# A hybrid decoder block on one core: the recurrence projected ahead of the convolution branch, two convolutions and ten weight tiles moved behind the opening of the last scan

## The chip, the core and the metric

The kernel runs on one core of a Trainium2 chip. The metric is device time in microseconds (us), from launch to end of one execution. Engines by their names in the profile: PE (matrix multiply; PEld is its weight load), DVE (vector), ACT (activations), POOL, and SP, which here only issues DMAs.

## The reference, cut to what matters

528 positions (16 learned ones and 512 of the input) with 1024 channels, one layer. `p = h @ W_in` has columns for three users:

```python
y_conv = conformer_conv(p[..., :2048], ...)      # GLU, causal depthwise conv of 31 taps, LayerNorm, silu, @ w_conv_out
y_rwkv = rwkv7_time_mix(p[..., 2048:5408], ...)  # 16 heads; S_t = S_{t-1} diag(w_t) + (S_{t-1} a_t) b_t^T + v_t k_t^T
gates  = sigmoid(p[..., 5408:] + b_gate)         # 2 x 1024 columns
y = gates[..., :1024] * y_conv + gates[..., 1024:] * y_rwkv
h = layer_norm(ALPHA * h + y @ w_o, ln1_g, ln1_b)
h = layer_norm(ALPHA * h + conv_gated_mlp(h, ffn_up, ffn_dw, ffn_down), ln2_g, ln2_b)
```

All of it is float32.

## The kernel before

Activations lie channels by positions, 128 channels to a tile. A product keeps float32 accuracy by three matmuls: weights and activations are each split into a high and a low part (`wh`, `wl`; `hhi`, `hlo`), and `gemm` (L167) sums high x high, low x high and high x low into one PSUM bank, for 8 blocks of 128 input channels. So one weight tile (128 output columns) against one half of the positions is 24 matmuls of 256 to 272 columns. A weight tile is loaded by SP into `wr` (two buffers), ACT writes `wh` (L153), DVE writes `wl` (L154). PSUM has eight banks: three `ps_g`, two `ps_x`, two `ps_a`, one `ps_m`.

The first phase works through steps that the string `SCHEDULE` (L50) names in program order. For a pair p of heads: `K` projects k, v, r (three weight tiles); `P` prepares the decays, keys and the matrices `Gt`; `S` (L505) inverts the triangular blocks in `Gt` by 61 dependent DVE instructions (L543 to L549), with a DRAM round trip on either side; `C` merges the inverse (L571) and runs the scan (L604), 9 dependent steps of small matmuls and copies through two `ps_x` banks; `F` (L647) normalises the scan's output in `ps_x` banks too and writes it to `o_dr`. For a channel tile j: `G` (L701) makes the GLU with two weight tiles; the convolution (L724) is 48 DVE instructions, either in between the steps of a solve (`S01`: solve of pair 0 with convolution 1) or by itself at low priority (`T`); it ends in `c_dr`. `A` (L751) makes one of 16 gate tiles with one weight tile and writes it to `g_dr`. `N` runs `conv_norm` (L768), the LayerNorm over channels of the convolution's output, which needs all eight tiles.

The string sets priorities and not the order. A planner orders each engine's instructions ahead of time: of those that could run by its own costs, the one first in program order goes first. `front()` puts instructions ahead of everything, `back()` behind, and `behind(ins, first)` forces one instruction behind another. On the chip each engine then runs its list in order. Weight preparation, the reads of PSUM after a `gemm`, and the scan are in `front()`. So PE, whenever the scan waits, takes matmuls from later `K`, `G` or `A` steps, if their inputs and buffers are there.

After the first phase: `w_conv_out` against the normalised convolution, times the first eight gates, to `ya_dr` (L834 to L844); `w_rwkv_out` against the scan's output, loaded from `o_dr` through two buffers, times the other eight gates, plus `ya` (L855 to L878); `w_o` in two halves of the positions, each followed by the first LayerNorm (L887 to L919); the up projection, 44 weight tiles (L932); the down projection (L981), which sums in all eight banks.

The functions that the diff touches, as they stand before:

Of the kernel before, what the change touches and what calls it, by code (L numbers as in the profile page):

```python
# [2 lines left out]

# [1 line left out]

# [37 lines left out]
GN_EPS = 64e-5  # L43
EXPM05 = float(np.exp(-0.5))
BACK = 3000
NKEEP = 6
GW = 132


SCHEDULE = ("G0 K0 P0 T0 G1 S01 K1 P1 C0 K2 F0 G2 S12 K3 P2 C1 G3 F1 K4 S23 G4 P3 C2 F2 A S34 K5 P4 C3 F3 G5 S4 A "  # L50
            "T5 K6 P5 G6 C4 F4 S56 P6 C5 K7 F5 G7 S67 A A A P7 C6 F6 S7 A A C7 A A N A A A A A A A F7")


@with_exitstack
def hybrid_block(ctx: ExitStack, tc: tile.TileContext, a, out, dbg=None):
# [108 lines left out]
    def wload(dram, c0, wpool=None, bufs=2):  # L164
        return wsplit(wcols(dram, c0), [P, NK, P], wpool, bufs)

    def gemm(ps, w, xh, xl, sl, nk=NK):  # L167
        wh, wl = w
        for k in range(nk):
            TE.matmul(ps, wh[:, k, :], xh(k, sl), start=(k == 0), stop=False)  # L170
            TE.matmul(ps, wl[:, k, :], xh(k, sl), start=False, stop=False)  # L171
            TE.matmul(ps, wh[:, k, :], xl(k, sl), start=False, stop=(k == nk - 1))  # L172

    hh = lambda k, sl: hhi[:, k, sl]
    hl = lambda k, sl: hlo[:, k, sl]
# [633 lines left out]
    for step in SCHEDULE.split():  # L809
        what, p, q = step[0], int(step[1:2] or 0), int(step[2:] or -1)  # L810
        if what == "K":
            raw[p] = rkv(p)
        elif what == "P":
            prs[p] = prep(p, *raw.pop(p))
        elif what == "S":
            solved[p] = solve(prs[p], conv(q, cpads.pop(q)) if q >= 0 else ())
        elif what == "C":
            with front():
                merge(prs[p], *solved[p])
                ys[p] = chain(prs[p])  # L820
        elif what == "F":
            finish(prs[p], ys.pop(p))
        elif what == "G":
            cpads[p] = glu(p)
        elif what == "T":
            with back():
                for _ in conv(p, cpads.pop(p)):
                    pass
        elif what == "A":
            gate(gates.pop(0))  # L830
        elif what == "N":
            ctx_a1.close()
            rb, zh, zl = conv_norm()
    for j in range(NK):  # L834
        ga = rb.tile([P, NQ], F32, name="ga", bufs=2)
        nc.sync.dma_start(out=ga, in_=g_dr[j])
        w = wload(a["w_conv_out"][0], P * j)
        for sl, n in qsl:
            pt = gbank()
            gemm(pt[:, :n], w, lambda k, s: zh[k][:, s], lambda k, s: zl[k][:, s], sl)  # L840
# [3 lines left out]
        nc.sync.dma_start(out=ya_dr[j], in_=ga)  # L844
    ctx_b1.close()
    ctx_a2.close()


    ctx_b2, ctx_o = ExitStack(), ExitStack()
    op = pool(ctx_o, "rout", "left")  # L850
    mp = pool(ctx_b2, "mix", "right")
    ot = lambda dt, name: op.tile([P, NQ], dt, name=name, tag="ot", bufs=16)
    yt = lambda dt, name: mp.tile([P, NQ], dt, name=name, tag="yt", bufs=16)
    oh, ol, yh, yl = [], [], [], []
    for j in range(NK):  # L855
        o_t = op.tile([P, NQ], F32, name="o_t", bufs=2)
        nc.sync.dma_start(out=o_t, in_=o_dr[j])
        oh.append(ot(F32R, "oh"))
        ol.append(ot(F32R, "ol"))
        split(oh[j], ol[j], o_t)  # L860
    for j in range(NK):
        gb_ = op.tile([P, NQ], F32, name="gb_", bufs=2)
        nc.sync.dma_start(out=gb_, in_=g_dr[8 + j])
        ya = op.tile([P, NQ], F32, name="ya", bufs=2)
        nc.sync.dma_start(out=ya, in_=ya_dr[j])
        w = wload(a["w_rwkv_out"][0], P * j)
        yh.append(yt(F32R, "yh"))
        yl.append(yt(F32R, "yl"))
        for sl, n in qsl:
            pt = gbank()  # L870
            gemm(pt[:, :n], w, lambda k, s: oh[k][:, s], lambda k, s: ol[k][:, s], sl)
            with front():
                V.scalar_tensor_tensor(out=gb_[:, sl], in0=gb_[:, sl], scalar=1.0, in1=pt[:, :n],
                                       op0=ALU.add, op1=ALU.mult)
# [12 lines left out]
    for (t0, t1), (sl, n) in zip(QH, qsl):  # L887
        pm, pv = abank(), abank()
        xs = []
        s1, s2 = half_tile("s1", n, 1), half_tile("s2", n, 1)  # L890
        for j in range(NK):
            w = kept[j] if j < NKEEP else wload(a["w_o"][0], P * j)
            pt = gbank()
            gemm(pt[:, :n], w, lambda k, s: yh[k][:, s], lambda k, s: yl[k][:, s], sl)
            x1 = half_tile("x1", n, 10)
            with front():
                V.scalar_tensor_tensor(out=x1, in0=hlo[:, j, t0:t1].bitcast(F32), scalar=ALPHA,
                                       in1=pt[:, :n], op0=ALU.mult, op1=ALU.add)
# [6 lines left out]
        with front():  # L905
# [7 lines left out]
            rs1 = mp.tile([P, 258], F32, name="rs1")[:, :n]  # L913
# [18 lines left out]
    def up_block(js):  # L932
# [107 lines left out]
```

## Time and profile before

| | |
|---|---|
| runs, us | 1180.61, 1184.78, 1188.44; median 1184.78 |
| profiled execution, us | 1186.58, its span 1184.5 |
| PE busy | 1131.2 us, 95% |
| DVE busy | 863.1 us, 73% |
| ACT busy | 565.0 us, 48% |
| mean granted PE clock | 0.979 of 2.4 GHz |

Times in the rows are microseconds from the start of the span; the first phase reaches to about 680, the two output projections to 750, the LayerNorm to 820, the up projection to 1057. Matmuls are pipelined: a busy PE can still be waiting inside, so the count of matmuls in a stretch is read beside its busy time.

### The profile page before, as it was taken

Reading aid. Unit: us, or ns where it says so; the run is one execution under the profiler, and the core shown is the slowest. Engines: PE = TensorE matmul, PEld = TensorE weight load, DVE = VectorE, ACT = ScalarE, POOL = GpSimd, SP = SyncE. Lnnn points to the kernel's source line nnn. Section 1 sums busy time; section 2 is a strip of 40 time slices with the busy share of each in tenths; the row PEclk is TensorE's granted clock in tenths of the full one; section 3 lists DMA queues with packets and bytes.
Section 4 is the critical chain, followed back from the end, with each engine's and each line's share of the span. In section 5 each row is a group of like instructions: output and inputs, shape, how many; then the busy total and the mean of one; then the engine's idle time right before and its main releaser. Section 6 shows DMA issues by size and latency. Waiting matters only on the chain.

```text
span 1184.5 us, 22671 instructions
## 1 busy us (share of the span) xinstructions
PE 1131.2 (95%) x8718; PEld 1066.5 (90%) x8718; DVE 863.1 (73%) x2179; ACT 565.0 (48%) x1211; POOL 83.2 (7%) x242
## 2 busy tenths in 40 slices
PE   5999999999999999999988999999999999999997
PEld 4998989899898989988977989998999999998885
DVE  6598999879898998976496447798876666652227
ACT  5644456537566565655585433346433443432120
POOL 6001010102101110101000000000000000000000
PEclk9999999999999999999898989999999999999999
DMA  5333342423414153344442376522332323343321
GB/s 161 86 89 91 86 95 63 93 57 90 100 55 107 42 108 81 80 119 107 128 134 77 98 223 191 166 71 75 105 106 74 107 74 106 90 137 95 94 84 71
DMA packets 202438, 118.99 MB, mean 100 GB/s; under 512 B 50036, under 2 KB 186397, under 8 KB 202331
## 3 DMA queue, kind: packets, MB, share of 16 engines
q1 hardware_dynamic: 182992, 113.81, 34.3%
q10 hardware_dynamic: 17515, 3.17, 1.5%
q8 instruction: 68, 1.11, 0.4%
q0 software_dynamic: 1824, 0.57, 0.3%
q14 instruction: 39, 0.32, 0.1%
HBM read 102.24 MB, written 15.28 MB: 99 GB/s over the span
## 4 chain that ended last, share of the span: by engine, by line
PE 64%; DVE 8%; DMA 5%; ACT 2%; issue 2%; POOL 0%; ACTq 0%; SPq 0%; DVEq 0%; POOLq 0%
PE ps_g L170 14%; PE ps_g L171 14%; PE ps_g L172 14%; PE ps_x L607 7%; PE psf L984 3%; PE psf L986 3%; PE psf L985 3%; DMA t22s<-dT 1%; PE ps_a L473 1%; PE ps_m L594 1%; DVE wl L154 1%; DMA dT<-W 1%; DMA t<-dT 1%; DMA wr<-in_ffn_up_dram 1%; DMA o_t<-o_dr 1%
## 5 line engine op out<-in xcount | busy, mean ns | idle before, releaser
L170 PE MATMUL ps_g<-hhi,wh 128*128 128x256 f32 (+2 forms) x1648 | 478.2, 290 | 4.7 <-DVE v L210 2.1
L171 PE MATMUL ps_g<-hhi,wl 128*128 128x256 f32 (+2 forms) x1648 | 478.2, 290 | 0.0
L172 PE MATMUL ps_g<-hlo,wh 128*128 128x256 f32 (+2 forms) x1648 | 476.2, 289 | 0.0
L170 PEld LDWEIGHTS ps_g<-hhi,wh 128*128 128x128 f32 x1648 | 314.1, 191 | 7.5 <-DVE v L210 2.5
L171 PEld LDWEIGHTS ps_g<-hhi,wl 128*128 128x128 f32 x1648 | 313.4, 190 | 2.8 <-issue 0.8
L172 PEld LDWEIGHTS ps_g<-hlo,wh 128*128 128x128 f32 x1648 | 314.0, 191 | 1.6 <-issue 0.6
L154 DVE TENSOR_TENSOR wl<-wr,wh 128x1024 fp32r<-128x1024 f32 x151 | 183.9, 1219 | 96.1 <-ACT wh L153 95.7
L153 ACT CAST wh<-wr 128x1024 fp32r<-128x1024 f32 x151 | 158.0, 1047 | 119.5 <-PE psf L985 75.2
L745 DVE SCALAR_TENSOR_TENSOR cev<-cd,drv,cev 128x257 f32<-128x257 f32 x216 | 99.0, 477 | 0.1
L942 ACT COPY pu<-ps_g 128x258 f32<-128x258 f32 (+1 forms) x88 | 32.8, 373 | 110.6 <-PE ps_g L172 110.6
L607 PE MATMUL ps_x<-UV,Gt 128*66 128x64 f32 (+1 forms) x576 | 71.1, 246 | 2.7 <-DMA Gt<-dT 2.3
L607 PEld LDWEIGHTS ps_x<-UV,Gt 128*66 128x66 f32 (+1 forms) x576 | 65.6, 168 | 4.4 <-DMA Gt<-dT 2.5
L984 PE MATMUL psf<-wh,hidh 128*128 128x512 f32 x176 | 69.3, 394 | 0.0
L986 PE MATMUL psf<-wl,hidh 128*128 128x512 f32 x176 | 69.0, 392 | 0.0
L985 PE MATMUL psf<-wh,hidl 128*128 128x512 f32 x176 | 68.3, 388 | 0.0
L949 DVE SCALAR_TENSOR_TENSOR u<-pu,prm,u 128x512 f32<-128x512 f32 x88 | 65.6, 747 | 1.3
L737 DVE SCALAR_TENSOR_TENSOR csh<-cpad,drv,csh 128x257 f32<-128x257 f32 x120 | 57.3, 477 | 0.5
L638 DVE SCALAR_TENSOR_TENSOR Sb<-Sb,lc,ps_x 64x64 f32<-64x64 f32 x112 | 31.3, 280 | 30.8 <-PE ps_x L607 29.2
L947 DVE TENSOR_SCALAR u<-pu,prm 128x512 f32<-128x512 f32 x44 | 21.2, 484 | 43.5 <-ACT pu L942 43.5
L547 DVE TENSOR_TENSOR stmp<-L,W 128x60 f32<-128x60 f32 (+21 forms) x216 | 45.1, 209 | 1.3
L549 DVE TENSOR_TENSOR W<-W,stmp 128x60 f32<-128x60 f32 (+21 forms) x216 | 45.0, 208 | 1.0
L170 PE MATMUL ps_g<-zh,wh 128*128 128x258 f32 (+1 forms) x128 | 38.4, 302 | 7.6 <-ACT zh L138 7.6
(308 smaller groups left out, 1992.2 us busy)
## 6 DMA issues: line engine op xcount, KB each, us to landing
wr<-in_w_in_dram SPq DMA_DIRECT2D x59, 512.0 KB, 4.3
wr<-in_ffn_up_dram SPq DMA_DIRECT2D x44, 512.0 KB, 4.0
wr<-in_ffn_down_dram SPq DMA_DIRECT2D x22, 512.0 KB, 3.6
wr<-in_w_o_dram SPq DMA_DIRECT2D x10, 512.0 KB, 4.4
g_dr<-gt SPq DMA_DIRECT2D x16, 257.0 KB, 3.0
L<-dA SPq DMA_DIRECT2D x32, 128.0 KB, 3.9
wr<-in_w_conv_out_dram SPq DMA_DIRECT2D x8, 512.0 KB, 4.2
wr<-in_w_rwkv_out_dram SPq DMA_DIRECT2D x8, 512.0 KB, 5.9
```

What stands on the lines that cost most here:

```text
L153: first = S.copy(out=hi, in_=raw)
L154: V.tensor_tensor(out=lo, in0=raw, in1=hi.bitcast(F32), op=ALU.subtract)
L170: TE.matmul(ps, wh[:, k, :], xh(k, sl), start=(k == 0), stop=False)
L171: TE.matmul(ps, wl[:, k, :], xh(k, sl), start=False, stop=False)
L172: TE.matmul(ps, wh[:, k, :], xl(k, sl), start=False, stop=(k == nk - 1))
L607: mm = lambda o, l, r, start: TE.matmul(o, l, r, start=start, stop=True, skip_group_check=True)
L737: yield V.scalar_tensor_tensor(out=cs_, in0=x1[:, i:i + NM], scalar=dcol(D_SCW, 8 * i + j) if i < HT else dcol(D_HCW, 8 * 2 * i + j), in1= ...
L745: yield V.scalar_tensor_tensor(out=yp[:, b, :] if lasttap else ev[:, b, :], in0=d[:, i:i + NM], scalar=dcol(D_HCW, 8 * (2 * i + b) + j), i ...
L949: V.scalar_tensor_tensor(out=u, in0=p_[:, t:t + SEQ], scalar=pcol(C_FW, 44 * t + m), in1=u, op0=ALU.mult, op1=ALU.add)
L984: TE.matmul(acc[t][d], hidh[:, k, ts], wd[k][0][:, ds], start=(k == 0), stop=False)
L985: TE.matmul(acc[t][d], hidl[:, k, ts], wd[k][0][:, ds], start=False, stop=False)
L986: TE.matmul(acc[t][d], hidh[:, k, ts], wd[k][1][:, ds], start=False, stop=(k == NF - 1))
```

## The change

The string: convolutions 0 to 5 stand in the solve of their own pair (`S00` to `S55`), 6 and 7 after everything of the last pair (`U6`, `U7`, at plain priority). `H` notes the first matmul of the last scan; from there to the end of the string every `gemm` puts its first matmul behind that one. Behind `H` stand the GLU tiles 6 and 7 and the last eight gates, four of them behind `U7`. `w_rwkv_out` comes next and writes gated `ya_dr`; then `conv_norm`; then `w_conv_out`, which adds `ya`. In these two stages the first two weight tiles are multiplied together, input block by input block, into four banks; the same is done for the second half of the positions in the up projection. The banks of a stage are taken in turn from `ps_g` and `ps_x`, or `ps_g` and `ps_a`. The scan's output gets 17 buffers in place of two for its loads. In the first LayerNorm `hhi + hlo` is added ahead of the product. Five tiles of `w_o` are kept for the second half, not six.

```diff
-NKEEP = 6
+NKEEP = 5
-SCHEDULE = ("G0 K0 P0 T0 G1 S01 K1 P1 C0 K2 F0 G2 S12 K3 P2 C1 G3 F1 K4 S23 G4 P3 C2 F2 A S34 K5 P4 C3 F3 G5 S4 A "
-            "T5 K6 P5 G6 C4 F4 S56 P6 C5 K7 F5 G7 S67 A A A P7 C6 F6 S7 A A C7 A A N A A A A A A A F7")
+SCHEDULE = ("G0 K0 P0 S00 K1 G1 P1 C0 K2 F0 S11 K3 P2 C1 G2 F1 K4 S22 P3 C2 G3 F2 A K5 S33 P4 C3 G4 F3 A K6 S44 P5 C4 "
+            "G5 F4 K7 S55 P6 C5 A F5 A S6 P7 C6 A F6 A S7 A A C7 H G6 G7 A A A A F7 U6 U7 A A A A")
+    hold = []
     def gemm(ps, w, xh, xl, sl, nk=NK):
         wh, wl = w
         for k in range(nk):
-            TE.matmul(ps, wh[:, k, :], xh(k, sl), start=(k == 0), stop=False)
+            first = TE.matmul(ps, wh[:, k, :], xh(k, sl), start=(k == 0), stop=False)
+            if k == 0 and hold:
+                behind(first, hold[-1], "work kept for the scan's waits")
...
+    def gemms(jobs, xh, xl, nk=NK):
+        for k in range(nk):
+            for ps, (wh, wl), sl in jobs:
+                TE.matmul(ps, wh[:, k, :], xh(k, sl), start=(k == 0), stop=False)
+                TE.matmul(ps, wl[:, k, :], xh(k, sl), start=False, stop=False)
+                TE.matmul(ps, wh[:, k, :], xl(k, sl), start=False, stop=(k == nk - 1))
+    turn, turn_a = cycle((gbank, xbank, gbank, xbank, gbank)), cycle((gbank, abank, gbank, abank, gbank))
+    obank = lambda: next(turn)()
+    cbank = lambda: next(turn_a)()
...
-        keys(X, 0, True)
+        opening = keys(X, 0, True)
...
+        elif what == "U":
+            for _ in conv(p, cpads.pop(p)):
+                pass
+        elif what == "H":
+            hold.append(opening)
...
+    ot = lambda dt, name: op.tile([P, NQ], dt, name=name, tag="ot", bufs=17)
...
+    for j in range(NK):
+        o_ts.append(ot(F32, "o_t"))
+        nc.sync.dma_start(out=o_ts[j], in_=o_dr[j])
...
+        if j < 2:
+            if j == 0:
+                first = [wload(a["w_rwkv_out"][0], P * i) for i in range(2)]
+                banks = [[obank()[:, :n] for sl, n in qsl] for i in range(2)]
+                gemms([(banks[i][x], first[i], qsl[x][0]) for i in range(2) for x in range(2)],
+                      lambda k, s: oh[k][:, s], lambda k, s: ol[k][:, s])
...
+        nc.sync.dma_start(out=ya_dr[j], in_=gb_)
+    ctx_a1.close()
+    rb, zh, zl = conv_norm()
...
-            V.tensor_tensor(out=ya[:, sl], in0=ya[:, sl], in1=gb_[:, sl], op=ALU.add)
+            V.tensor_tensor(out=ya[:, sl], in0=ya[:, sl], in1=ga[:, sl], op=ALU.add)
...
-            pt = gbank()
+            pt = obank()
+            x1 = half_tile("x1", n, 12)
+            V.tensor_tensor(out=x1, in0=hhi[:, j, t0:t1].bitcast(F32), in1=hlo[:, j, t0:t1].bitcast(F32), op=ALU.add)
             gemm(pt[:, :n], w, lambda k, s: yh[k][:, s], lambda k, s: yl[k][:, s], sl)
-            x1 = half_tile("x1", n, 10)
             with front():
-                V.scalar_tensor_tensor(out=x1, in0=hlo[:, j, t0:t1].bitcast(F32), scalar=ALPHA,
-                                       in1=pt[:, :n], op0=ALU.mult, op1=ALU.add)
-                V.scalar_tensor_tensor(out=x1, in0=hhi[:, j, t0:t1].bitcast(F32), scalar=ALPHA,
-                                       in1=x1, op0=ALU.mult, op1=ALU.add)
+                V.scalar_tensor_tensor(out=x1, in0=x1, scalar=ALPHA, in1=pt[:, :n], op0=ALU.mult, op1=ALU.add)
...
-        for sl, n in qsl:
-            for x in ws:
-                pt = gbank()
-                gemm(pt[:, :n], wt[x], lambda k, s: h1h[:, k, s], lambda k, s: h1l[:, k, s], sl)
+        for i_, (sl, n) in enumerate(qsl):
+            pts = [obank() for x in ws]
+            jobs = [(pt[:, :n], wt[x], sl) for pt, x in zip(pts, ws)]
+            for some in [jobs] if i_ else [[job] for job in jobs]:
+                gemms(some, lambda k, s: h1h[:, k, s], lambda k, s: h1l[:, k, s])
```

## Rows read from the trace of the kernel before

**Rows 1.** Stretches: length; busy (count) of PE, PEld, DVE, ACT, POOL; clock, DMA, GB/s

```profile
60.00:500.00 440.00, 429.70 (x3496) 404.08 (x3495) 396.43 (x1242) 248.39 (x597) 51.29 (x140) 0.98 0.33 82
500.00:608.00 108.00, 104.40 (x844) 96.74 (x844) 73.02 (x249) 65.22 (x165) 7.50 (x23) 0.95 0.46 119
600.00:640.00 40.00, 29.24 (x210) 27.68 (x210) 34.58 (x94) 29.23 (x58) 1.69 (x2) 0.83 0.28 77
618.00:632.00 14.00, 5.22 (x22) 4.58 (x21) 13.86 (x39) 9.19 (x15) 0.00 (x0) 0.57 0.12 37
640.00:680.00 40.00, 40.00 (x341) 37.80 (x341) 17.09 (x45) 18.09 (x45) 0.00 (x0) 1.00 0.37 117
680.00:720.00 40.00, 37.09 (x284) 36.45 (x283) 20.32 (x37) 13.34 (x20) 0.00 (x0) 0.91 0.74 218
776.00:824.00 48.00, 43.27 (x349) 42.17 (x348) 41.09 (x92) 27.10 (x60) 0.00 (x0) 1.00 0.19 54
820.00:840.00 20.00, 20.00 (x171) 20.00 (x170) 18.49 (x26) 10.74 (x17) 0.00 (x0) 1.00 0.46 132
1080.00:1100.00 20.00, 20.00 (x89) 16.43 (x88) 3.68 (x3) 4.02 (x4) 0.00 (x0) 1.00 0.36 106
```

**Rows 2.** Waits of PE from 600 to 640: total us, times, longest

```profile
PE ps_g L170 <- ACT zh L138: 7.6, 1, 7.6
PE ps_a L795 <- DVE qsum L792: 1.8, 1, 1.8
```

**Rows 3.** The chain that ended last, from 676 to 702: start, us, what

```profile
683.59 6.17 DMA ya_dr<-ga
...
690.70 3.98 DMA o_t<-o_dr
```

**Rows 4.** Waits of PE from 776 to 824

```profile
PE ps_g L170 <- DVE x L897: 1.8, 1, 1.8
```

**Rows 5.** Reads of the gates' banks from 606 to 644: start, us

```profile
608.15 0.46 ACT L759 ACTIVATE gt<-ps_g,drv 128x256 f32<-128x256 f32 x1
...
615.39 0.47 ACT L759 ACTIVATE gt<-ps_g,drv 128x256 f32<-128x256 f32 x1 [1.47 <-PE ps_g L172]
```

**Rows 6.** Timeline of PE from 606 to 609, the scan's matmuls

```profile
608.15 0.40 PE L607 MATMUL ps_x<-UV,Gt 128*66 128x64 f32 x4
```

**Rows 7.** Timeline of DVE from 606 to 609

```profile
607.33 0.22 DVE L549 TENSOR_TENSOR W<-W,stmp 128x68 f32<-128x68 f32 x1
607.51 0.76 DVE L695 TENSOR_TENSOR on<-ps_x,on 128x258 f32<-128x258 f32 x2
```

**Rows 8.** DVE groups over the span: xcount, busy us, mean ns, idle before

```profile
L154 DVE TENSOR_TENSOR wl<-wr,wh 128x1024 fp32r<-128x1024 f32 x151 | 183.9, 1219 | 96.1 <-ACT wh L153 95.7
L745 DVE SCALAR_TENSOR_TENSOR cev<-cd,drv,cev 128x257 f32<-128x257 f32 x216 | 99.0, 477 | 0.1
...
L787 DVE TENSOR_TENSOR c_t<-c_t,ps_a 128x258 f32<-128x258 f32 (+1 forms) x16 | 6.6, 414 | 0.1
...
L842 DVE SCALAR_TENSOR_TENSOR ga<-ga,ps_g 128x258 f32<-128x258 f32 (+1 forms) x16 | 6.6, 418 | 6.2 <-PE ps_g L172 6.2
...
L800 DVE TENSOR_TENSOR c_t<-c_t,rstd 128x514 f32<-128x514 f32 x8 | 5.5, 689 | 0.0
L141 DVE TENSOR_TENSOR zl<-c_t,zh 128x514 fp32r<-128x514 f32 x8 | 5.5, 689 | 3.0 <-ACT zh L138 2.9
...
L792 DVE TENSOR_TENSOR qsum<-qsum,csq 128x514 f32<-128x514 f32 x7 | 4.8, 685 | 0.0
L780 DVE TENSOR_TENSOR csum<-csum,c_t 128x514 f32<-128x514 f32 x6 | 4.1, 690 | 0.0
...
L797 DVE RECIPROCAL rstd<-rstd 128x258 f32<-128x258 f32 (+1 forms) x2 | 3.5, 1750 | 0.0
```

**Rows 9.** Steps of the solve (L549 alone) in two solves: DVE busy, count, clock

```profile
326.00:370.00 44.00, 5.55 (x27) 1.00 0.27 74
526.00:549.00 23.00, 5.72 (x27) 1.00 0.28 81
```

More of the change, by code (lines that the diff above doesn't have):

```diff
@@ L1 @@
 from contextlib import ExitStack, nullcontext
-from itertools import chain as chain_
+from itertools import chain as chain_, cycle
 import numpy as np
@@ L612, in keys @@
         def keys(X, c, start):
-            for h in range(2):
-                mm(X[0:66, at(0, h)], Gt[:, h, c, 0:66], UV[:, c, half[h]], start and h == 0)
+            return [mm(X[0:66, at(0, h)], Gt[:, h, c, 0:66], UV[:, c, half[h]], start and h == 0) for h in range(2)][0]
         X = xbank()
-        keys(X, 0, True)
+        opening = keys(X, 0, True)
         for c in range(NCH):
@@ L644, in chain @@
             X = Xn
-        return Y
+        return Y, opening
     def finish(pr, Y):
@@ L819, in hybrid_block @@
                 merge(prs[p], *solved[p])
-                ys[p] = chain(prs[p])
+                ys[p], opening = chain(prs[p])
         elif what == "F":
@@ L828, in hybrid_block @@
                     pass
+        elif what == "U":
[3 more added lines that the diff above has]
+            hold.append(opening)
         elif what == "A":
             gate(gates.pop(0))
-        elif what == "N":
-            ctx_a1.close()
-            rb, zh, zl = conv_norm()
-    for j in range(NK):
-        ga = rb.tile([P, NQ], F32, name="ga", bufs=2)
-        nc.sync.dma_start(out=ga, in_=g_dr[j])
-        w = wload(a["w_conv_out"][0], P * j)
-        for sl, n in qsl:
-            pt = gbank()
-            gemm(pt[:, :n], w, lambda k, s: zh[k][:, s], lambda k, s: zl[k][:, s], sl)
+    hold.clear()
@@ new lines, in hybrid_block @@
+    ctx_a2.close()
+    ctx_o = ExitStack()
+    op = pool(ctx_o, "rout", "left")
+    ot = lambda dt, name: op.tile([P, NQ], dt, name=name, tag="ot", bufs=17)
+    oh, ol = [], []
+    o_ts = []
+    for j in range(NK):
+        o_ts.append(ot(F32, "o_t"))
+        nc.sync.dma_start(out=o_ts[j], in_=o_dr[j])
+    for j in range(NK):
+        oh.append(ot(F32R, "oh"))
+        ol.append(ot(F32R, "ol"))
+        split(oh[j], ol[j], o_ts[j])
+    for j in range(NK):
+        gb_ = op.tile([P, NQ], F32, name="gb_", bufs=2)
+        nc.sync.dma_start(out=gb_, in_=g_dr[8 + j])
+        if j < 2:
[4 more added lines that the diff above has]
+                      lambda k, s: oh[k][:, s], lambda k, s: ol[k][:, s])
+        else:
+            w = wload(a["w_rwkv_out"][0], P * j)
+        for x, (sl, n) in enumerate(qsl):
+            if j < 2:
+                pt = banks[j][x]
+            else:
+                pt = obank()
+                gemm(pt[:, :n], w, lambda k, s: oh[k][:, s], lambda k, s: ol[k][:, s], sl)
+            with front():
+                V.scalar_tensor_tensor(out=gb_[:, sl], in0=gb_[:, sl], scalar=1.0, in1=pt[:, :n],
+                                       op0=ALU.add, op1=ALU.mult)
+        nc.sync.dma_start(out=ya_dr[j], in_=gb_)
@@ new lines, in hybrid_block @@
+    ctx_a1.close()
+    rb, zh, zl = conv_norm()
+    ctx_o.close()
+    ctx_f, ctx_b2 = ExitStack(), ExitStack()
+    fw = pool(ctx_f, "upw", "left")
+    mp = pool(ctx_b2, "mix", "left")
+    yt = lambda dt, name: mp.tile([P, NQ], dt, name=name, tag="yt", bufs=16)
+    yh, yl = [], []
+    for j in range(NK):
+        ga = mp.tile([P, NQ], F32, name="ga", bufs=2)
+        nc.sync.dma_start(out=ga, in_=g_dr[j])
+        ya = mp.tile([P, NQ], F32, name="ya", bufs=2)
+        nc.sync.dma_start(out=ya, in_=ya_dr[j])
+        if j < 2:
+            if j == 0:
+                first = [wload(a["w_conv_out"][0], P * i) for i in range(2)]
+                banks = [[cbank()[:, :n] for sl, n in qsl] for i in range(2)]
+                gemms([(banks[i][x], first[i], qsl[x][0]) for i in range(2) for x in range(2)],
+                      lambda k, s: zh[k][:, s], lambda k, s: zl[k][:, s])
+        else:
+            w = wload(a["w_conv_out"][0], P * j)
+        yh.append(yt(F32R, "yh"))
+        yl.append(yt(F32R, "yl"))
+        for x, (sl, n) in enumerate(qsl):
+            if j < 2:
+                pt = banks[j][x]
+            else:
+                pt = cbank()
+                gemm(pt[:, :n], w, lambda k, s: zh[k][:, s], lambda k, s: zl[k][:, s], sl)
@@ L843, in hybrid_block @@
                                        op0=ALU.add, op1=ALU.mult)
[L844 to L869, printed above, removed]
-            pt = gbank()
[L871 to L874, printed above, removed]
-            V.tensor_tensor(out=ya[:, sl], in0=ya[:, sl], in1=gb_[:, sl], op=ALU.add)
+            V.tensor_tensor(out=ya[:, sl], in0=ya[:, sl], in1=ga[:, sl], op=ALU.add)
             S.activation(out=yh[j][:, sl], in_=ya[:, sl], func=AF.Copy, scale=0.5)
@@ L878, in hybrid_block @@
                                    op0=ALU.mult, op1=ALU.subtract)
-    ctx_o.close()
+    ctx_b1.close()
     h1h, h1l = hhi[:, :, Q0:T], hlo[:, :, Q0:T]
-    ctx_f = ExitStack()
-    fw = pool(ctx_f, "upw", "left")
+    ctx_n = ExitStack()
+    lnp = pool(ctx_n, "norm1", "right")
     kept = [wload(a["w_o"][0], P * j, mp, bufs=NKEEP) for j in range(NKEEP)]
-    half_tile = lambda name, n, bufs: mp.tile([P, 258], F32, name=name, bufs=bufs)[:, :n]
+    half_tile = lambda name, n, bufs: lnp.tile([P, 258], F32, name=name, bufs=bufs)[:, :n]
     for (t0, t1), (sl, n) in zip(QH, qsl):
@@ L892, in hybrid_block @@
             w = kept[j] if j < NKEEP else wload(a["w_o"][0], P * j)
-            pt = gbank()
+            pt = obank()
+            x1 = half_tile("x1", n, 12)
+            V.tensor_tensor(out=x1, in0=hhi[:, j, t0:t1].bitcast(F32), in1=hlo[:, j, t0:t1].bitcast(F32), op=ALU.add)
             gemm(pt[:, :n], w, lambda k, s: yh[k][:, s], lambda k, s: yl[k][:, s], sl)
-            x1 = half_tile("x1", n, 10)
             with front():
-                V.scalar_tensor_tensor(out=x1, in0=hlo[:, j, t0:t1].bitcast(F32), scalar=ALPHA,
-                                       in1=pt[:, :n], op0=ALU.mult, op1=ALU.add)
-                V.scalar_tensor_tensor(out=x1, in0=hhi[:, j, t0:t1].bitcast(F32), scalar=ALPHA,
-                                       in1=x1, op0=ALU.mult, op1=ALU.add)
+                V.scalar_tensor_tensor(out=x1, in0=x1, scalar=ALPHA, in1=pt[:, :n], op0=ALU.mult, op1=ALU.add)
             xs.append(x1)
@@ L912, in hybrid_block @@
             TE.matmul(pv[:, :n], ones_d, s2, start=True, stop=True)
-            rs1 = mp.tile([P, 258], F32, name="rs1")[:, :n]
+            rs1 = lnp.tile([P, 258], F32, name="rs1")[:, :n]
             S.activation(out=rs1, in_=pv[:, :n], func=AF.Sqrt, bias=eps_ln)
@@ L923, in hybrid_block @@
     fl = ExitStack()
+    ctx_n.close()
     ctx_b2.close()
@@ L936, in up_block @@
         pu = {x: up.tile([P, NQ], F32, name="pu", bufs=4) for x in ws}
-        for sl, n in qsl:
-            for x in ws:
-                pt = gbank()
-                gemm(pt[:, :n], wt[x], lambda k, s: h1h[:, k, s], lambda k, s: h1l[:, k, s], sl)
+        for i_, (sl, n) in enumerate(qsl):
[3 more added lines that the diff above has]
+                gemms(some, lambda k, s: h1h[:, k, s], lambda k, s: h1l[:, k, s])
+            for pt, x in zip(pts, ws):
                 with front():
```

## The prediction

> **What bounds the kernel now.** I read the busy times by stretch first, then PE's waits in the stretches where PE is not full, then the DVE groups. Three pictures come out of the stretches. From 60 to 500 PE is busy 429.7 of 440 us and DVE 396.4, 90% [rows 1]: both are nearly full, so only work taken away or moved can shorten it. From 500 to 608 DVE falls to 73.0 of 108 while PE stays at 104.4: no convolution is left, and PE lives on gates and small matmuls. Behind that come three holes on PE. From 600 to 640 it is busy 29.24 of 40. The wait is 7.6 us for the first normalised tile `zh`, after 1.8 for `qsum` [rows 2]: all gates are spent (the last is read at 615.39 [rows 5]) while DVE, full in 618 to 632 (13.86 of 14), still normalises. From 680 to 720 PE is short by 2.9 us: the chain shows a store of `ya`, 6.17, and behind it a load of `o_t`, 3.98 [rows 3]. From 776 to 824, the first LayerNorm, it is short by 4.7; the longest named wait is 1.8, for a bank that DVE has not read yet [rows 4]. From 640 to 680 DVE is busy only 17.09 of 40. The up projection is full: 171 matmuls in 20 us, 0.117 each.
>
> **The change part by part**, against the profiled execution's own 1186.6 us (span 1184.5); the median of the runs stands 1.8 lower.
>
> *Recurrence first.* With `w_rwkv_out` ahead of `conv_norm`, 8 x 2 x 24 matmuls x 0.117 = 45 us of PE work cover the normalisation. What goes is 40 - 29.24 = 10.8 idle plus the clock: in 618 to 632 the granted clock is 0.57, which is 86% of that time at 1.2 GHz, with 5.22 us of matmuls in it, half of which, 2.6, is loss. Together -13.4. The `o_t` hole goes too: eight loads have buffers of their own, and the four gates behind `U7` (4 x 48 x 0.117 = 22 us) cover the last store and load, 6.2 + 4.0. That is 2.9 idle, and a clock of 0.91 over 40 us, 7.2 us at 1.2 GHz, some 4.3 of them busy, so 2.1: -5.0. SP runs its list in order; should the load of the last `o_t` or of the last convolution, each waiting for its store, stand ahead of weight loads, up to 10.2 would come back. I take 0 while that cover is there.
>
> *Work moved behind the opening.* The opening of the last scan is its first small matmul, at 608.15, as pair 6's last two multiplies (607.51, 0.76 long) release a `ps_x` bank [rows 6, 7]. Of the gates' 32 half tiles three are read at 608.15 or later (the first and the last of them stand in [rows 5]), so 14.5 gates are done by then. In the changed string eight stand ahead. So PE loses 6.5 x 48 x 0.117 = 36.5, and two GLU tiles of 96 matmuls, 22.5: 59 us. DVE loses two convolutions, 48 instructions of 0.477 each, at most 46, and 10.5 weight parts of 1.219 [rows 8], 12.8: also 59. By throughput of either engine the opening comes at 608 - 59 = 549. Nothing but the recurrence's own latency can hold it later, and what the rows show is that a solve's length follows DVE's load: the same 27 steps, 5.55 and 5.72 us of DVE, take a stretch of 44 us with DVE loaded and one of 23 with no convolution about [rows 9]. I take +3 for PE without filler ahead of the opening; the ends are 0 and +40 (an opening that moves by only some 20).
>
> *The tail behind the opening.* PE has 22.5 + 8 x 5.6 + 45 = 112 us of weight tiles up to `w_conv_out`, and some 10 of the scan (my estimate; the rows don't separate it): 122. DVE has two convolutions 46, `conv_norm` 30.0 (6.6 + 5.5 + 5.5 + 4.8 + 4.1 + 3.5), 20 weight parts 24.4, 16 bank reads 6.7, eight splits of the scan's output (as `zl`, 5.5), the last solve about 15 (the step row's pair of 27 twice, 11.3, and 19 others): 128 [rows 8, 9]. DVE ends second by 6, its durations overlap a little, and `zh` comes tile by tile, so the four banks can use it as it comes: +2, ends 0 and +11. This is the cover of *Recurrence first*; without it the hole is back.
>
> *First tiles over four banks.* Where the input blocks come one by one, PE has up to 12 matmuls per block (1.4 us), and a bank more than three. With the single PSUM read in the LayerNorm in place of two, and five banks for the 1.8 us bank wait, I take 2 of the 4.7: -2, ends -4.7 and 0. In the up projection the second halves run two weights in turn for 44 x 24 x 0.117 = 124 us. Per column the up stretch costs 20/171/257 = 0.455 ns, the down projection, which changes its bank every three matmuls, 20/89/512 = 0.439. So 0, ends -4.4 and +4.4.
>
> The Trainium skill speaks against the turning banks: TensorE: Matmul & The Clock Gate, section "A second HAM failure mode: psum-queue depth-cycling", tells of a kernel that cycled through PSUM banks and idled PE between groups, so that its clock swung between the levels. Here the trace disagrees: with eight banks in turn the down projection has clock 1.00 at 20.00 busy of 20 [rows 1].
>
> *Fewer kept `w_o`.* One more weight preparation: 1.2 on DVE beside a stage where DVE is busy 41 of 48: +0.5, ends 0 and +2.3 (with as much on ACT).
>
> Sum: -13.4 - 5.0 + 3 + 2 - 2 + 0.5 = -14.9. That is 1171.7 for the profiled execution, **1170** for the median.
>
> **The rivals.**
>
> *The scan's latency holds the opening.* Place: the last three pairs, where nothing is left to fill PE but eight gates. From 500 to 608 DVE was no bound (68%); PE was full there only because of gates that now stand behind `H`. If the loop of scan, preparation, solve and merge keeps its length, each us by which the opening comes after 549 is a us of idle PE, at a lower clock besides. It decides from 14.9 + 3 = 18 us on, an opening at 567: from there it is slower than before. At 580 it gives 1170 + 28 = 1198. Against it: DVE's 59 us fewer over the loop's whole length. Chance 0.19.
>
> *DVE late at `w_conv_out`.* The hole moves instead of closing: 128 against 122 with the convolutions started only when GLU 6 is out, and weight parts ahead of them in priority. 11 us more, some at 1.2 GHz: about 1182. For it: DVE at 13.86 of 14 when it did this alone. Chance 0.19.
>
> *The tie does not do what it says.* It hangs on the scan's first step, which needs only its first chunk; at 608.15 the last solve was still running (a step of it at 607.33 [rows 7]). So the kept tiles may be spent before the last scan's waits begin: some 10 us, 1180. Chance 0.06.
>
> *The banks in turn cost clock.* If a third of the 124 us ran at 1.2 GHz: +41, 1211. The trace speaks against it. Chance 0.02. The Trainium skill's TensorE: Matmul & The Clock Gate has this rule, in the section named above.
>
> **How the numbers follow.** The forecast has 0.54, by itself 1156 to 1176. A measurement of this kernel tells about 1% from no change, so faster means under 1172.9 and slower over 1196.6. Faster: 0.48 of the forecast and 0.02 of a mild late DVE, 0.50. Same: the rest of the forecast 0.06, late DVE 0.17, the tie 0.06, a mild late opening 0.04: 0.33. Slower: 0.15 late opening, 0.02 banks: 0.17. The low end has every gain at its bound, 13.4 + 5.0 + 4.7 + 4.4 = 27.5, so 1157, and part of the 10.3 us that PE idles from 60 to 500: 1150. The high end takes the late DVE and half of the late opening: 1194.
>
> **What would show it.** Right: the opening near 550; PE full from there to the end of `w_conv_out`, without a wait for `zh` or `oh` over 3 us, and a clock of 1.00; DVE over 90% busy over that stretch and the `conv_norm` groups inside the `w_rwkv_out` stage; the 1.8 bank wait gone; 0.117 per matmul in the up projection. Wrong: PE under 95% ahead of the opening, with waits for merge, scan and preparation, at clocks below 1 (late opening); a wait for `zh` of 7 us again (late DVE); gates ending before the last scan's second step (the tie); a clock under 1 past 820 (banks).

## The result and the profile after

The changed kernel takes **1218.93 us** (median of four runs, 1217.56 to 1223.07), the kernel before 1184.47 beside it: ratio of the runs 1.0316, 95% interval 1.0282 to 1.0351 (the two medians alone give 1.029). It is slower by 3%, where 1170 was forecast. The profiled execution took 1217.56 us, its span 1215.5, with a mean granted clock of 0.958.

The stretches of the changed kernel, PE, PEld, DVE, ACT and POOL busy with counts, then clock, DMA share and GB/s, beside [rows 1]:

```profile
60.00:480.00 420.00, 412.35 (x3426) 389.75 (x3424) 372.86 (x1177) 247.48 (x604) 51.91 (x146) 1.00 0.36 87
480.00:580.00 100.00, 77.43 (x419) 63.97 (x419) 54.49 (x220) 44.64 (x131) 7.15 (x19) 0.62 0.14 31
580.00:660.00 80.00, 80.00 (x678) 77.73 (x677) 60.87 (x143) 34.83 (x76) 0.00 (x0) 1.00 0.37 100
660.00:680.00 20.00, 9.63 (x56) 8.52 (x55) 14.62 (x28) 6.39 (x13) 0.00 (x0) 0.71 0.93 314
870.00:1070.00 200.00, 200.00 (x1694) 200.00 (x1693) 138.25 (x190) 79.79 (x141) 0.00 (x0) 1.00 0.33 94
```

Up to 480 PE is as full as before. Then it is bare for 100 us: 419 matmuls, at a clock of 0.62. The kernel before did 777 in the same 100 us, at 0.95:

```profile
480.00:580.00 100.00, 96.56 (x777) 89.22 (x776) 70.95 (x243) 60.80 (x157) 10.14 (x29) 0.95 0.42 100
```

DVE is no bound there either, 54.49 of 100. The second hole, 660 to 680, leaves PE idle for 10.4 us, as much as the one of 600 to 640 did before (10.8), but for other waits. PE's waits of the changed kernel, first in 480 to 580, and below the mark in 655 to 740 (total, times, longest):

```profile
PE ps_x L686 <- ACT Y L682: 9.7, 6, 5.3
PE ps_x L625 <- ACT UV L646: 4.8, 12, 0.7
PE ps_x L625 <- ACT Rz L643: 4.5, 12, 0.6
...
PE ps_a L802 <- DVE csum L797: 6.9, 1, 6.9
PE ps_g L183 <- ACT oh L139: 3.5, 1, 3.5
```

The first three are the recurrence waiting for itself: PE's transposes of the scan's output (L686) for its normalisation on ACT, and the scan's matmuls (L625) for copies of the step before. No wait for `zh` is left; `csum`, the sum that `conv_norm` starts with, and `oh` have taken its place. Three timelines of the changed kernel (start, us) answer to [rows 5 to 7]: the last gate half tile read ahead of the last scan (ACT), its opening (PE, L625 is L607 of before) and the last gate read (ACT):

```profile
487.80 0.47 ACT L776 ACTIVATE gt<-ps_g,drv 128x256 f32<-128x256 f32 x1
...
573.51 0.71 PE L625 MATMUL ps_x<-UV,Gt 128*66 128x64 f32 x4 [0.56 <-DVE on L712]
...
664.49 0.47 ACT L776 ACTIVATE gt<-ps_g,drv 128x256 f32<-128x256 f32 x1 [2.29 <-PE ps_g L177]
```

All eight free gates are spent at 488. The opening comes at 573.5, 34.6 us earlier than before, where 59 had been moved behind it.

### The profile page after: what moved, and what is told of

Read it like the earlier page. It is cut to its first block, busy times and chain, and to the rows that moved or that the text cites. A ratio compares the mean times of both kernels' runs of the same rounds, so it can differ in the third digit from the quotient of the medians.

```text
span 1215.5 us, 22672 instructions
## 1 busy us (share of the span) xinstructions
PE 1147.1 (94%) x8718; PEld 1078.6 (89%) x8718; DVE 877.4 (72%) x2180; ACT 563.6 (46%) x1212; POOL 82.2 (7%) x242
## 4 chain that ended last, share of the span: by engine, by line
PE 66%; DVE 8%; DMA 3%; ACT 3%; issue 2%; SPq 0%; ACTq 0%; DVEq 0%; POOL 0%
PE ps_x L625 8%; PE ps_g L176 6%; PE ps_g L173 6%; PE ps_g L177 6%; PE ps_g L183 4%; PE ps_g L184 4%; PE ps_g L185 4%; PE ps_x L183 3%; PE psf L1037 3%; PE psf L1036 3%; PE ps_x L184 3%; PE ps_x L185 3%; PE psf L1038 3%; PE ps_a L491 1%; DVE wl L155 1%
## 5 line engine op out<-in xcount | busy, mean ns | idle before, releaser
L173 PE MATMUL ps_g<-hhi,wh 128*128 128x256 f32 (+2 forms) x944 | 278.8, 295 | 0.5 <-DVE r L228 0.4
L176 PE MATMUL ps_g<-hhi,wl 128*128 128x256 f32 (+2 forms) x944 | 278.3, 295 | 0.0
L177 PE MATMUL ps_g<-hlo,wh 128*128 128x256 f32 (+2 forms) x944 | 276.5, 293 | 0.0
L177 PEld LDWEIGHTS ps_g<-hlo,wh 128*128 128x128 f32 x944 | 180.4, 191 | 1.5 <-issue 0.6
L183 PE MATMUL ps_g<-hhi,wh 128*128 128x256 f32 (+1 forms) x424 | 120.3, 284 | 0.0
L184 PE MATMUL ps_g<-hhi,wl 128*128 128x256 f32 (+1 forms) x424 | 119.8, 282 | 0.4 <-DVE wl L155 0.4
L185 PE MATMUL ps_g<-hlo,wh 128*128 128x256 f32 (+1 forms) x424 | 119.4, 282 | 0.0
L183 PE MATMUL ps_x<-hhi,wh 128*128 128x256 f32 (+1 forms) x280 | 79.8, 285 | 4.1 <-ACT hhi L139 4.1
L625 PE MATMUL ps_x<-UV,Gt 128*66 128x64 f32 (+1 forms) x576 | 77.5, 261 | 5.0 <-DMA Gt<-dT 3.0
L185 PEld LDWEIGHTS ps_g<-hlo,wh 128*128 128x128 f32 x424 | 80.3, 190 | 0.0
L184 PE MATMUL ps_x<-hhi,wl 128*128 128x256 f32 (+1 forms) x280 | 79.3, 283 | 0.0
L185 PE MATMUL ps_x<-hlo,wh 128*128 128x256 f32 (+1 forms) x280 | 79.2, 283 | 0.0
L625 PEld LDWEIGHTS ps_x<-UV,Gt 128*66 128x66 f32 (+1 forms) x576 | 72.2, 183 | 7.6 <-DMA Gt<-dT 3.2
```

The source lines that it names most:

```text
L173: first = TE.matmul(ps, wh[:, k, :], xh(k, sl), start=(k == 0), stop=False)
```

## The experiments

**Theory 1, the tie**: the latency of the recurrence holds the opening, so work tied behind it leaves PE bare ahead of it. **Theory 2, the string**: the convolutions' new places make the recurrence or the tail late, tie or no tie. Theories 3 and 4 are put in the runs that test them. Each kernel was timed against the one before on the same chip; these are medians, and ratios to before with their intervals.

| run | us | ratio |
|---|---|---|
| changed kernel | 1218.93 | 1.0316 (1.0282 to 1.0351) |
| no_tie | 1197.5 | 1.0156 (1.0130 to 1.0181) |
| tie_gates | 1210.64 | 1.0266 (1.0241 to 1.0291) |
| gt_apart | 1220.7 | 1.0347 (1.0318 to 1.0375) |
| old_string | 1210.46 | 1.0264 (1.0230 to 1.0299) |
| conv_first | 1166.62 | 0.9888 (0.9841 to 0.9934) |
| conv_first_back | 1166.59 | 0.9889 (0.9839 to 0.9938) |
| other_o | 1195.93 | 1.0136 (1.0089 to 1.0182) |
| other_c | 1219.69 | 1.0335 (1.0276 to 1.0394) |
| free_queue | 1196.71 | 1.0136 (1.0115 to 1.0158) |
| conv_first_tail | 1166.45 | 0.9891 (0.9867 to 0.9914) |

**no_tie**: nothing tied. Here and below only the part of a line that differs is shown.

```diff
-S7 A A C7 H G6 G7 A A A A F7 U6 U7 A A A A
+S7 A A C7 G6 G7 A A A A F7 U6 U7 A A A A
```

> The changed kernel without the H in its string: GLU tiles 6 and 7 and the last eight gates may fill PE before the last scan's opening. Theory 1 (the tie starves PE: the recurrence sets the opening at 574, and from 488 to 578 PE has only small matmuls at 1.2 GHz): PE full from 488 to 574 at clock 1.00, the opening where it was within 10 us, convolutions 6 and 7 done by then, and 1180 to 1195. Theory 2 (convolutions in their own pair's solve slow the recurrence, the tie is harmless): 1210 to 1220, a hole ahead of the opening that stays.

Measured 1197.5: theory 2's 1210 to 1220 fell, theory 1's range was missed by 2.5. Its stretches, columns as above:

```profile
540.00:580.00 40.00, 39.91 (x344) 38.25 (x343) 37.22 (x126) 21.58 (x53) 1.94 (x4) 1.00 0.40 111
...
600.00:620.00 20.00, 16.09 (x88) 13.40 (x87) 8.78 (x20) 5.80 (x18) 0.00 (x0) 0.65 0.56 165
620.00:640.00 20.00, 13.38 (x60) 11.44 (x60) 12.46 (x39) 9.04 (x22) 0.00 (x0) 0.50 0.00 0
640.00:660.00 20.00, 8.66 (x28) 6.52 (x29) 15.36 (x25) 16.06 (x31) 0.00 (x0) 0.50 0.44 145
```

And DVE's last product of pair 6, which releases the opening (start, us):

```profile
577.37 0.76 DVE L712 TENSOR_TENSOR on<-ps_x,on 128x258 f32<-128x258 f32 x2
```

PE is full ahead of the opening, and pair 6 is finished at 578, against 574 in the changed kernel. A full PE or a bare one at a clock of 0.62 makes 4 us of difference: what fills PE does not set the opening, the recurrence's own chain does. But now PE is bare behind it, at 600 to 660, and the kernel is still slower than before. The last solve shared DVE with convolution 7, and the last merge began at 599.3, against 583.7 in the changed kernel.

**tie_gates**: the GLU tiles free, the last gates tied.

```diff
-S7 A A C7 H G6 G7 A A A A F7
+S7 G6 G7 A A C7 H A A A A F7
```

> The changed kernel with GLU tiles 6 and 7 ahead of the opening and free, the last eight gates still tied. Theory 1: 23 us of matmuls move into the hole before the opening, and convolutions 6 and 7 into DVE's idle time there (7 to 12 of 20 us busy): 1188 to 1202. Theory 2: 1210 to 1220.

Measured 1210.64, a miss for theory 1 and just inside theory 2's range: in 540 to 580 PE is busy 26.72 of 40 at 0.50, with a wait of 9.6 for `t11n`, the solved block that a merge starts from, here pair 6's. And what theory 2 says of the convolutions happened here: untied, the GLU tiles let convolutions 6 and 7 start early, and they ran for the most part in the last two solves. The steps of these solves (the 27 of [rows 9]: DVE busy, count, clock, DMA share, GB/s), first in the changed kernel, below the mark in tie_gates:

```profile
498.00:517.00 19.00, 5.58 (x27) 0.68 0.00 1
553.00:574.00 21.00, 5.87 (x27) 0.50 0.00 0
...
500.00:538.00 38.00, 5.62 (x27) 1.00 0.29 73
561.00:597.00 36.00, 6.05 (x27) 0.50 0.12 37
```

The opening came at 594.4, 21 us later than in the changed kernel. So this run does not price the tie of the gates by itself: it changes the load on the chain too.

**gt_apart**: a gate's tile, which is stored by SP, in a pool that stays open, so that what reuses the scan's memory needn't wait for the gates.

```diff
-gt = sp.tile([P, NQ], F32, name="gt", bufs=2)
+gt = cp.tile([P, NQ], F32, name="gt", bufs=2)
```

> The changed kernel with the gate tile gt in the constants' pool and not in the scan's. Theory 3 (the second hole, 665 to 677 and a slow clock to 682, comes because the loads of o_t reuse the scan's memory and wait for the last gate's store): o_t is loaded by 655, no wait for oh over 2 us, 10 to 14 us less, 1205 to 1209. Rival (SP's list puts the loads of c_t ahead anyway): no change, 1216 to 1221.

Measured 1220.7, no gain. PE's longest waits in 640 to 760 show why: `oh` is gone, `zh` is there.

```profile
PE ps_g L183 <- ACT zh L139: 8.3, 1, 8.3
```

DVE did not hold `zh`: it was busy 8.31 of the 20 us from 700 to 720. The sum `qsum` that `conv_norm` needs was ready at 698.2, and PE multiplied it 17 us later, with no idle time in front of it: in PE's list it stands behind matmuls of `w_rwkv_out`. The rows of `qsum` (duration in ns; first and last start, us):

```profile
L809 DVE TENSOR_TENSOR qsum<-qsum,csq x7: 684/689/696, 691.5 to 697.5; 128x514 f32<-128x514 f32 x7
L812 PE MATMUL ps_a<-qsum,ones_d x4: 377/380/383, 715.4 to 716.1; 128*128 128x258 f32 x2, 128*128 128x256 f32 x2
```

**old_string**: all of the change but the string, which is that of before without `N`; nothing tied.

> The changed kernel with the string of before, less its N: convolutions where they were, nothing tied, all else as changed (recurrence first, banks, kept tiles). Theory 2: far faster than no_tie, 1165 to 1180. Theory 1: about no_tie, within 8 us, since the tie is the cost and not the place of the convolutions.

Measured 1210.46. Theory 2 fell, as in no_tie, this time by 30 us. Theory 1 missed too, by 13 to no_tie: the string of the change is the better one. With the string of before and no tie, the rest of the change costs 2.6%. What is left is the order of the two projections with what was built for it (the loads' 17 buffers, the first tiles over four banks), and the change's last part, which conv_first_tail prices.

**conv_first**: the kernel before, its order of projections and its banks, with the changed string's first part.

```diff
-G5 S4 A T5 K6 P5 G6 C4 F4 S56 P6 C5 K7 F5 G7 S67 A A A P7 C6 F6 S7 A A C7 A A N A A A A A A A F7
+G5 F4 K7 S55 P6 C5 G6 F5 S66 P7 C6 G7 F6 S77 A A C7 A A N A A A A A A A A A A F7
```

> The kernel before with the new string alone, untied: convolutions in the solve of their own pair for all eight pairs, GLU 6 and 7 in their places, N ahead of the last gates, w_conv_out first as before. Theory 4 (the order of the two projections is the loss: with the recurrence first only K, G and A can fill PE until the last scan is projected, with the convolution first w_conv_out fills it too): faster than before, 1160 to 1178, since the string alone brings the sixth scan's end from 595 to about 565. Rival (the string itself is worse): 1185 to 1200.

Measured 1166.62: faster than before by 1.1%, and the fastest of all with its two relatives. Its stretches:

```profile
600.00:620.00 20.00, 11.62 (x54) 9.17 (x55) 14.84 (x29) 12.67 (x29) 1.32 (x2) 0.57 0.27 62
620.00:640.00 20.00, 20.00 (x181) 19.22 (x180) 10.75 (x28) 11.82 (x30) 0.00 (x0) 1.00 0.18 54
640.00:660.00 20.00, 20.00 (x167) 19.39 (x166) 9.49 (x23) 10.34 (x21) 0.00 (x0) 1.00 0.51 149
```

PE is full from 620 on, through the last scan and the store and load behind it, on `w_conv_out`. Two rows show what the order is worth, with the last start behind "to": the last product of the recurrence on DVE, and ACT's split `yh`, the end of the second projection. First conv_first, then the changed kernel, then no_tie, one fence each:

```profile
L695 DVE TENSOR_TENSOR on<-ps_x,on x16: 413/418/428, 202.9 to 654.1; 128x258 f32<-128x258 f32 x8, 128x256 f32<-128x256 f32 x8
L876 ACT ACTIVATE yh<-ya x16: 408/418/423, 683.7 to 728.6; 128x258 fp32r<-128x258 f32 x8, 128x256 fp32r<-128x256 f32 x8
```

```profile
L712 DVE TENSOR_TENSOR on<-ps_x,on x16: 414/418/427, 202.6 to 644.7; 128x258 f32<-128x258 f32 x8, 128x256 f32<-128x256 f32 x8
L927 ACT ACTIVATE yh<-ya x16: 410/420/423, 742.2 to 781.2; 128x258 fp32r<-128x258 f32 x8, 128x256 fp32r<-128x256 f32 x8
```

```profile
L712 DVE TENSOR_TENSOR on<-ps_x,on x16: 364/415/430, 201.7 to 649.3; 128x258 f32<-128x258 f32 x8, 128x256 f32<-128x256 f32 x8
L927 ACT ACTIVATE yh<-ya x16: 409/420/423, 721.7 to 760.8; 128x258 fp32r<-128x258 f32 x8, 128x256 fp32r<-128x256 f32 x8
```

From the last product to the last `yh` conv_first takes 74.5 us (before 72.5), no_tie 111.5 (old_string 111.9), the changed kernel 136.5. Convolution first, one projection runs beside the last scan and only the other is left behind it. Recurrence first, both are left, and nothing but gates and GLU tiles covered the last scan. No run changes the order alone: conv_first differs from no_tie in the last part of the string, the buffers and the banks too.

**conv_first_back**: the same with convolutions 6 and 7 by themselves at low priority (`T6`, `T7`).

> As conv_first, but convolutions 6 and 7 at the lowest priority and not in between the steps of the last two solves. Theory 4: as conv_first or up to 10 us less (1155 to 1178), since the last two solves stay short. Rival: 1185 to 1200.

1166.59, the same. The last two solves did not stay short: they took 39 and 38 us, as in conv_first (39 and 35). PE still waits 8.1 us for `t11n`, from 605 to 613: the gates are spent (the last is read at 602) when the last solve ends.

**other_o**: no_tie with the loads of `o_t` from pairs 0 to 5 only.

```diff
-nc.sync.dma_start(out=o_ts[j], in_=o_dr[j])
+nc.sync.dma_start(out=o_ts[j], in_=o_dr[min(j, 5)])
```

> The untied changed kernel (no_tie), in which the projection of the recurrence reads pair 5's stored output in place of those of pairs 6 and 7, so it waits for neither of the last two scans; both are still computed and stored. Theory 4: the stretch from 600 to 660, where PE is bare at 1.2 GHz, is filled by w_rwkv_out, and 15 to 30 us go, 1165 to 1182. Rival (the bare stretch comes from DVE or from weights): 1190 to 1198, as no_tie.

1195.93, a miss: the wait for `oh` stays at 10.3. The data of the last pairs are not what holds the projection. **other_c** is the same for `conv_norm`'s loads, on gt_apart.

```diff
-nc.sync.dma_start(out=c_t, in_=c_dr[j])
+nc.sync.dma_start(out=c_t, in_=c_dr[min(j, 5)])
```

> gt_apart, in which the normalisation reads convolution 5's stored output in place of those of 6 and 7; both are still computed and stored. Theory (in gt_apart the hole before w_rwkv_out only moved to w_conv_out, because convolution 7 ends late: zh waits 8.3): the wait for zh goes and 8 to 14 us with it, 1206 to 1213. Rival (gt_apart lost its gain to something else, as DMA traffic): 1218 to 1222.

1219.69, a miss as well; the wait for `zh` stays at 8.3. In both cases something else than the data of the last pairs holds the projection: in other_c it is PE's list, as in gt_apart, with `qsum` ready at 698.3 and multiplied at 715.5. In no_tie, and in other_o alike, SP's queue stands at the last pair's store. SP of no_tie (start, us):

```profile
649.82 0.32 SPq L713 DMA_DIRECT2D o_dr<-on  x1
650.19 4.14 SPq L863 DMA_DIRECT2D o_t<-o_dr  x8
```

and its wait there, 39.3 in other_o:

```profile
SPq L713 <- DVE on L712: 41.0, 1, 41.0
```

So **free_queue**: other_o with that store on POOL's queue.

```diff
-nc.sync.dma_start(out=o_dr[p], in_=on)
+nc.gpsimd.dma_start(out=o_dr[p], in_=on)
```

> This is `other_o` (nothing tied; the eight loads of the scan's output read pairs 0 to 5 only, so what is projected last isn't the reference's) with the store of the scan's output issued from POOL's queue in place of SP's. In `other_o` SP's queue stood 39 us at that store, waiting for the last pair's last product, and the o_t loads stand behind it in SP's list. Theory A, the list held them: without the store SP issues them from about 610, the recurrence's projection starts its first seven input blocks inside the last scan, the 10 us wait for oh goes, and the time is 1175 to 1187 against 1195.9. Theory B, their memory held them (the tiles lie where the last pair's inputs still are): some load waits for the last pair's matmuls at about 648, the ones behind it in the list with it, the oh wait stays over 5 us and the time is 1191 to 1199.

1196.71, theory B's range. SP reaches the loads at 614 and stands among them instead, at the third; SP's row in the timeline:

```profile
614.11 38.40 SPq L863 DMA_DIRECT2D o_t<-o_dr  x8
```

and the waits of SP and of PE:

```profile
SPq L863 <- DVE on L704: 34.3, 1, 34.3
...
PE ps_g L183 <- ACT oh L139: 10.3, 1, 10.3
```

A load that needs nothing of the last pair waits for DVE's L704, the addition just ahead of that pair's last product. It isn't the data and it isn't the store in SP's list. The pool of the `o_t` tiles opens where the scan's has closed, so the tile lies where the scan still works. The loads behind it wait with it. But the loads are not all that holds PE: the first of them landed at 619.5, and ACT split it only at 659.0, behind the first four of `conv_norm`'s `zh` in its list:

```profile
L139 ACT CAST oh<-o_t x8: 607/620/625, 659.0 to 666.2; 128x514 fp32r<-128x514 f32 x8
```

**conv_first_tail**: conv_first with the change's last part, the first LayerNorm and the up projection.

```diff
-NKEEP = 6
+NKEEP = 5
...
-            pt = gbank()
+            pt = obank()
+            x1 = half_tile("x1", n, 12)
+            V.tensor_tensor(out=x1, in0=hhi[:, j, t0:t1].bitcast(F32), in1=hlo[:, j, t0:t1].bitcast(F32), op=ALU.add)
...
-        for sl, n in qsl:
+        for i_, (sl, n) in enumerate(qsl):
+            pts = [obank() for x in ws]
```

> conv_first (1166.6) with the changed kernel's last part alone: one PSUM read in the first LayerNorm with hhi + hlo added ahead, five kept tiles of w_o, banks in turn from ps_g and ps_x, and in the up projection the second halves multiplied together. By the prediction's terms -2 + 0.5 + 0: 1165, with ends 1158 to 1173. By the trace of the changed kernel (first LayerNorm 0.7 longer, up projection 0.4 longer) it is worth nothing: 1165 to 1169, and the granted clock stays at 1.00 past 820 either way. If the banks in turn cost clock, the up stretch shows under 1.00 and the time is over 1175.

1166.45, worth nothing against conv_first's 1166.62, as read from the changed kernel. The stretch of the LayerNorm and then the 256 us to just past the end of the up projection, conv_first in the first fence, conv_first_tail in the second:

```profile
729.00:780.00 51.00, 48.51 (x392) 47.58 (x392) 43.26 (x94) 20.80 (x37) 0.00 (x0) 1.00 0.34 97
780.00:1036.00 256.00, 253.88 (x2127) 252.96 (x2126) 180.16 (x261) 110.82 (x200) 0.00 (x0) 1.00 0.32 92
```

```profile
729.00:780.00 51.00, 50.96 (x416) 50.39 (x415) 40.48 (x86) 23.01 (x43) 0.00 (x0) 1.00 0.38 110
780.00:1036.00 256.00, 250.75 (x2089) 249.04 (x2088) 176.54 (x254) 107.50 (x195) 0.00 (x0) 0.99 0.32 90
```

The LayerNorm's bank wait goes, 24 more matmuls run in its stretch, and 38 fewer run behind it: the gain is given back at the start of the up projection, where PE waits 2.8 for its first input blocks `hhi` (1.7 without the change) and its clock from 780 to 800 is 0.91.

## Why the prediction was wrong

The account, of one execution against the other: the profiled time was forecast as 1171.7 and is 1217.56, 45.9 more. The opening came at 573.5 instead of 552: 21.5. The stretch behind it, up to the last `yh`, first in the changed kernel and below the mark before:

```profile
573.50:782.00 208.50, 197.26 (x1579) 192.52 (x1580) 143.56 (x289) 87.04 (x157) 0.87 (x2) 0.95 0.52 153
...
608.00:751.00 143.00, 129.33 (x1024) 125.18 (x1023) 84.84 (x188) 64.31 (x123) 1.69 (x2) 0.93 0.51 151
```

At 0.117 for each matmul 23.8 us are lost there where before lost 23.2, and I had expected 16.4 of those to go: 17.0 more than forecast. The 555 more matmuls are 51 more than the 504 I had moved: 6.0. From the last `yh` to the down projection's first matmul it took 305.1 us (to 1086.3) against 304.8 (to 1055.2), where 1.5 was to be gained: 1.8. Together 46.3; these are estimates, as the small matmuls of the scan are counted like the others.

**Work moved behind the opening** is the step that failed first: "Nothing but the recurrence's own latency can hold it later", at a price of 3. It did hold it, and the price was 25. The rows that I drew on were two solves [rows 9], 44 us and 23 us long; I let the loop shorten with DVE's load. The solves did follow it: the changed kernel's last two lie within 19 and 21 us. But a solve is one part of a round, from one pair's last product to the next pair's, and the loop as a whole hardly got shorter. The last product of pairs 2 and 4, before:

```profile
358.18 0.76 DVE L695 TENSOR_TENSOR on<-ps_x,on 128x258 f32<-128x258 f32 x2
...
490.01 0.76 DVE L695 TENSOR_TENSOR on<-ps_x,on 128x258 f32<-128x258 f32 x2
```

and of pairs 2, 4 and 6 in the changed kernel:

```profile
328.48 0.76 DVE L712 TENSOR_TENSOR on<-ps_x,on 128x258 f32<-128x258 f32 x2
...
461.28 0.76 DVE L712 TENSOR_TENSOR on<-ps_x,on 128x258 f32<-128x258 f32 x2
...
573.02 0.76 DVE L712 TENSOR_TENSOR on<-ps_x,on 128x258 f32<-128x258 f32 x2
```

Before, pair 6 follows at 607.51 [rows 7]: four rounds in 249.3 us, the last two of them in 117.5. In the changed kernel the four took 244.5 and the last two 111.7, though DVE was busy for only 64.67 us of these. The last round took 56.0 us there and 54.0 before, and no round of any run was under 51.1 (old_string): an opening at 552 would have asked for two of 45 behind the changed kernel's pair 4. What the string gave, 30 us, it gave in the first three pairs. This was the first rival, in mechanism: it named the place, and said from which opening on the kernel is slower, 567. By it an opening at 573.5 would give 1170 + 21.5, some 1191; the remaining 27 are the next steps'.

**Recurrence first** gave the holes back. The `zh` hole went, as forecast. But the `o_t` hole, which was to vanish behind "the four gates behind `U7`", became the main one: 9.63 busy of 20 us from 660 to 680. The gates did run there, and the last store of the scan's output, at 645.2, was long done; the loads were issued only at 668.4, behind the last gate's store at 665.0, the loads of `c_t` and a weight load that waited for its buffer, and the block `oh` came at 676. PE spent most of that time, 6.9 us, at `csum`, whose matmuls stand ahead of `oh` in its list. I had given each load a buffer of its own in mind, and not asked where the buffers lie. In gt_apart, with the gates' tile out of the scan's memory, the loads were issued from 645.8 on, right behind the last store; but then `zh` was late by 8.3, and nothing was gained.

What the step overlooked altogether is larger: `w_conv_out` is 45 us of PE work that needs nothing of the last pairs, and before it ran beside the last scan (640 to 680, full, in [rows 1]). Put last, it can't. By old_string, less the change's last part, which conv_first_tail shows to be worth nothing on another string, recurrence first costs 2.6%, about 31 us; how much of that is the order and how much the place of the buffers and PE's and ACT's lists, no run separates. By conv_first a string much like the change's gains 1.1%, 13. Their product, 1.0149, is close to no_tie's 1.0156; as the two strings differ in their last part, that is a sign and no proof. The tie adds 1.0316 / 1.0156, 1.6% or some 20 us. I took the gates and GLU tiles to be as good a cover as the projection; they were cover ahead of the opening already, and spending them behind it opens the hole in front.

**The tail behind the opening**: DVE was not late at `w_conv_out` (+2 forecast; no wait for `zh`). Right, but for the reason that PE was later still. gt_apart, with PE earlier, has the wait that the second rival foretold, but not by its mechanism: DVE had idle time, and PE's list held the norm.

**First tiles over four banks**: the 1.8 bank wait went, and -2 did not come: the wait for the up projection's first `hhi` grew from 1.7 to 4.1, and conv_first_tail shows the same by itself, 1.7 to 2.8. The 0.5 for *Fewer kept `w_o`* is in these stretches and was not told apart.

```profile
PE ps_x L183 <- ACT hhi L139: 4.1, 1, 4.1
```

In the up projection 0 was right: 1694 matmuls in 200 us, and 1689 in 850 to 1050 before, both at a clock of 1.00. Turning banks didn't cost clock in this stretch. The Trainium skill's TensorE: Matmul & The Clock Gate, section "A second HAM failure mode: psum-queue depth-cycling", tells of bank cycling in which PE idles briefly between the groups of matmuls. Here PE was busy 200.00 of 200 us, so this stretch does not bear on that case, for or against.

**The tie does not do what it says** fell: no gate is read between 488 and the opening.

What stays open: how much of the 31 us would be left if the recurrence's inputs had memory of their own and their splits and the norm's matmuls stood earlier in the lists of ACT and PE. That wasn't tried.

## What to carry to other kernels

Work that fills an engine while a serial chain runs is worth what the chain leaves idle: count what may run beside the last round of the chain, and put the largest stage that doesn't need it there. Before forecasting that a chain ends earlier, measure its rounds from end to end, several in a row, and not one stage of it. A load with a buffer of its own can still wait for the last user of the memory that the buffer lies in, and what stands behind it in its queue waits too, as in free_queue for 34.3 us. When a wait names a tile, see when its inputs were ready: in gt_apart `qsum` stood ready for 17 us behind other matmuls in PE's list.

## What was not expected of the hardware

The bare recurrence runs at the low clock though PE counts as busy most of the time. The changed kernel's stretches:

```profile
520.00:540.00 20.00, 18.20 (x103) 14.84 (x102) 7.33 (x26) 10.11 (x30) 3.25 (x11) 0.62 0.34 72
540.00:560.00 20.00, 16.00 (x82) 13.57 (x81) 7.77 (x34) 4.62 (x18) 0.49 (x1) 0.56 0.01 1
```

91% and 80% busy, at 0.62 and 0.56 of 2.4 GHz, so mostly at 1.2. A busy share near full was no sign of a full clock here; the matmuls of these stretches are the recurrence's small ones. And the chain of the recurrence hardly noticed: its round from 517.0 to 573.0 took 56.0 us at a clock of 0.56, and the one from 553.5 to 607.5 before took 54.0 at 0.94.
